# Sharing the last PSUM eviction of a block inversion between two engines, in a two-layer hybrid encoder

## The chip, the cores and the metric

The kernel runs on one core of a Trainium2 chip. The metric is the device time of one execution in microseconds (us). TensorE multiplies matrices into PSUM, VectorE and ScalarE read PSUM and work on SBUF, GpSimd does a few small powers, SyncE issues the DMAs.

## The reference, cut to what matters

Two layers, 256 tokens, width 2048. A layer is a norm, one input projection, two groups of heads, their gates, one output projection and a residual:

```
h = rms_norm(x); proj = h @ w_in
r, k, v, xw, xa = bidir_token_shift(...)      # 16 heads of 64, RWKV-7, two directions
S = S * w_t - (S kk_t) (a_t kk_t)^T + v_t k_t^T ;  y_t = S r_t     # per head, per direction
q, k_at, v_at -> rope -> windowed attention with a sink            # 16 query heads, 4 key heads
x = x + concat(y_rw * silu(g_rw), y_at * silu(g_at)) @ w_out
```

The change lies in the recurrence. The kernel computes it in chunks of 64 tokens. Inside a chunk the delta rule needs the inverse of a unit triangular 64 x 64 matrix for each head, direction and chunk.

## The kernel before, in words

**The weight stream.** The two projections are TensorE's bulk. Each weight tile is loaded as f32 (`raw`) and split by `wsplit` (line 217) into a high part `hi` (ScalarE, line 222) and the rest `lo` (VectorE, line 224), in two halves of 512 columns; three matmuls a step multiply them (`pm`, lines 292 to 294).

**Windows and slots.** `layer` (line 655) walks windows of 64 weight steps, each cut into 12 slots (`window`, line 394). At the head of each slot pieces of other work are put in, then the slot's 5 or 6 weight steps follow. The pieces are Python generators, one `yield` a piece. `scans` (line 1019) says which generator of which pair of heads advances at which slots:

- `scan_p` (line 690) prepares a pair: decays, keys, and a bonus `bv`. It has 13 pieces. `STAGE_P0` (line 47) gives the slots of the first pair, in windows 0 and 1; its last pieces come in window 2 by `STAGE_P[1]` (line 46), as for every pair.
- `scan_i` (line 776) builds a pair's chunk matrices and inverts them: matmuls `pg` for direction 0 and then 1, each masked by VectorE into `ge` (line 792) and copied in part to `AB` by ScalarE; `pt` (lines 807 and 815) and level 0 of the inversion (`pq`, line 886); five more levels (`pq`, `pd`, line 905, and VectorE's masked copy into `TC`, line 907); then a last correction. It takes all 12 slots of its window and slots 0 and 1 of the next.
- `scan_b` (line 938) runs the recurrence over the chunks, one or two windows later.

**The last correction.** `pf` (line 909) is a pair of PSUM banks. `turn` (line 860) puts the transposed columns of the last level into columns 256 to 383 of both banks; the matmuls of lines 914 to 919 put sums into columns 0 to 255. ScalarE copies the sums to `FN` (line 921) and the transposed columns to `TT` (the function `turned` that `turn` returns, line 867). A slot later `pn` (line 925) multiplies `FN` and `TT`.

**Buffers.** `pf`, `pg`, `pt`, `pq`, `pd`, `pn`, `pbn` and others are tiles of one pool of bank pairs, `ps_w`, with two buffers (line 151). `pf` of a pair stands in slot 0 of a window, and straight behind it come the two `pg` of the next pair.

**Order.** TensorE's order is the program's own (line 142). The order of the other engines is set when the program is built, by a list scheduler that goes by program position; `tc.high_priority(offset=n)` moves an instruction n places ahead (`PRIO_TC` is 400, line 59). `PA` and `PV` (line 239) are ScalarE and VectorE with program order kept among themselves.

In the trace the tiles have the names of their tags: `TC` is `tv`, `TT` is `tt`, `FN` is `q`, `GE` is `ge`, `BK` is `bk`.

Of the kernel before, what the change touches and what calls it, by code (L numbers as in the profile page):

```python
# [15 lines left out]
AF = mybir.ActivationFunctionType  # L16
# [5 lines left out]
T = 256  # L22
# [21 lines left out]
SLOTS = 12  # L44

STAGE_P = (([5], [3, 4, 5, 6, 7, 8, 9, 10, 11]), ([2], [0, 2]))
STAGE_P0 = (([], [10, 11]), ([2], [2, 4, 5, 7, 8, 9, 10, 11]))
STAGE_I = (list(range(SLOTS)), [0, 1])
STAGE_B = (list(range(1, 12)), [0, 1, 2, 3, 4, 5])
ATT = [  # L50
# [8 lines left out]
PRIO_TC = 400  # L59
# [75 lines left out]
def hybrid_trunk_kernel(ctx, tc, xT, wi, wv, wo, par, fing, dup, iup, sink, pos, cst, out):  # L135
    nc = tc.nc
    V, A, G, PE, SY = nc.vector, nc.scalar, nc.gpsimd, nc.tensor, nc.sync
# [15 lines left out]
    def wpair(name):  # L153

        return ps_w.tile([128, 2, 512], F32, tag="w", name=name)
# [4 lines left out]
    def st(tag, shape, dt=F32, bufs=1):  # L160
        return sp.tile([128, *shape], dt, tag=tag, name=tag, bufs=bufs)

    def pick(t, rows, off, *dims):

        a = t[rows]
        return bass.AP(tensor=a.tensor, offset=a.offset + off, ap=[a.ap[0], *dims])

    every = slice(0, 128)
# [486 lines left out]
    def layer(l):  # L655
# [120 lines left out]
        def scan_i(p, t):  # L776
# [75 lines left out]
            TT = st("tt", [2, NC, 64], F16)  # L852
# [7 lines left out]
            def turn(ps, b):  # L860

                for d, c, h in dch:
                    PE.matmul(
                        ps[half[h ^ d], d, c * 32 : (c + 1) * 32], hq(TC, d, c, h),
                        pick(EYE, half[h], (1 - d) * b, [2 * b, 32 // b], [1, b]), start=True, stop=True,
                    )
                return lambda: A.activation(  # L867
                    pick(TT, every, b, [T - b, 2], [2 * b, 128 // b], [1, b]), ps.rearrange("p d (n b) -> p d n b", b=b), AF.Copy
                )

            for li, b in enumerate(LEVELS):

# [22 lines left out]
                for d, c, h in dch:  # L895
                    PE.matmul(narrow(pq[:, d], h ^ d, c), hq(AB, d, c, h), sub(TC, h, d, c, d * b), start=True, stop=True)  # L896
                turned = li > 1 and turn(pq[:, :, 128:256], LEVELS[li - 1])

                A.activation(t_sub(QF), flat4(pq[:, :, 0:128]), AF.Copy)
# [8 lines left out]
                yield  # L908
            pf = wpair("pf")
            turned = turn(pf[:, :, 256:384], LEVELS[-1])  # L910
            o = lambda d, c, h: pf[half[h ^ d], d, c * 64 : (c + 1) * 64]
            for d in range(2):
# [5 lines left out]
                PE.matmul(o(d, c, h), hq(AB, d, c, h), hq(TC, d, c, h), start=False, stop=False, skip_group_check=True)  # L918
                PE.matmul(o(d, c, h), hq(AL, d, c, h), hq(TC, d, c, h), start=False, stop=True, skip_group_check=True)
            FN = st("q16", [2, NC, 64], F16)  # L920
            A.activation(FN.rearrange("p d c j -> p d (c j)"), pf[:, :, 0:T], AF.Copy)
            turned()
            yield

            pn = wpair("pn")
# [93 lines left out]
        def scans(w):  # L1019

            gens = []
            prep = [(w, STAGE_P0[w])] if w < 2 else [(2, STAGE_P[1]), (1, STAGE_P[0])]
            stages = [(lag, scan_p, at[0]) for lag, at in prep]
            stages += [(4, scan_b, STAGE_B[1]), (3, scan_i, STAGE_I[1]), (3, scan_b, STAGE_B[0])]
            stages += [(2, scan_i, STAGE_I[0])]
            stages += [(lag, scan_p, at[1]) for lag, at in prep]
            for lag, scan, at in stages:
                p = w - lag
                if 0 <= p < NP:
                    if (scan, p) not in chains:  # L1030
                        chains[scan, p] = scan(p, L.ts[p])
                    gens.append((chains[scan, p], at))
            return gens
# [210 lines left out]
```

## Time and profile before

| | us |
|---|---|
| median of 3 runs (lowest, highest) | 1191.46 (1190.85, 1194.27) |
| the profiled execution | 1191.11 |
| its span, first to last instruction | 1189.3 |
| TensorE matmuls busy | 1152.2 (97%) |
| VectorE busy | 910.1 (77%) |
| ScalarE busy | 792.6 (67%) |

All durations are of the one profiled execution. Engines: PE is TensorE (PEld its weight loads), DVE is VectorE, ACT is ScalarE, POOL is GpSimd, SP is SyncE. A row of the timeline has the start in us from the span's start, the duration, the engine, the line, the operation, what is written from what, the shape and a count; in brackets stand the engine's idle time before it and what ended it. The granted TensorE clock was 0.993 of full speed over the span.

### The profile page before, as it was taken

What the parts mean: (1) busy time and instruction counts of PE and PEld (TensorE: products, weight loads), DVE (VectorE), ACT (ScalarE), POOL (GpSimd) and SP (SyncE); (2) the same over time, 40 slices, a digit from 0 to 9 for tenths busy, and PEclk for the clock granted to TensorE, in tenths of its full rate; (3) what the DMA queues carried; (4) which work ended last, traced back from release to release, by engine and by line L of the source; (5) the groups of instructions that cost most, each with busy time, mean ns of one, the idle gap of its engine ahead of it and who ended that gap; (6) DMA issues with size and microseconds to landing.
All of it is one profiled execution on the core that took longest, in us unless ns stands there. A gap on an engine that the chain in (4) does not pass through costs nothing.

```text
span 1189.3 us, 38176 instructions
## 1 busy us (share of the span) xinstructions
PE 1152.2 (97%) x16151; PEld 1081.0 (91%) x16151; DVE 910.1 (77%) x2017; ACT 792.6 (67%) x1987; POOL 20.7 (2%) x23
## 2 busy tenths in 40 slices
PE   8999999999999999999999999999999999999996
PEld 6988988898898989899999888988898899989996
DVE  7889878988877678766678888878887767786554
ACT  6657776777777566655555777776777766765553
POOL 0000000000000000000000000000000000000000
PEclk9999999999999999999999999999999999999998
DMA  7553333333333434477654433333333344346663
GB/s 256 165 169 123 110 106 115 112 96 112 108 95 119 138 116 136 143 236 238 207 184 166 135 123 115 99 108 115 112 102 100 117 135 124 113 147 190 212 187 120
DMA packets 60410, 166.63 MB, mean 140 GB/s; under 512 B 7728, under 2 KB 22736, under 8 KB 60240
## 3 DMA queue, kind: packets, MB, share of 16 engines
q1 hardware_dynamic: 60240, 164.21, 43.1%
q8 instruction: 126, 2.06, 0.7%
q14 instruction: 44, 0.36, 0.1%
HBM read 157.37 MB, written 4.19 MB: 136 GB/s over the span
## 4 chain that ended last, share of the span: by engine, by line
PE 67%; issue 16%; DVE 7%; ACT 7%; DMA 2%; SPq 0%; POOL 0%; DVEq 0%; POOLq 0%; ACTq 0%
PE pm L292 17%; PE pm L293 14%; PE pm L294 14%; DVE lo L224 3%; ACT hi L222 2%; PE pcc L952 2%; PE pcc L978 2%; PE pg L786 1%; PE py L959 1%; DMA raw<-wi 1%; PE pq L896 1%; PE pd L905 1%; ACT ysq L996 1%; PE pcc L965 1%; PE py L985 1%
## 5 line engine op out<-in xcount | busy, mean ns | idle before, releaser
L292 PE MATMUL pm<-XH,hi 128*128 128x256 f32 x1664 | 490.7, 295 | 1.2 <-ACT XH L184 0.8
L294 PE MATMUL pm<-XH,lo 128*128 128x256 f32 x1664 | 468.3, 281 | 2.9 <-DVE lo L224 2.9
L293 PE MATMUL pm<-XL,hi 128*128 128x256 f32 x1664 | 467.7, 281 | 0.8 <-DVE XL L185 0.6
L224 DVE TENSOR_TENSOR lo<-raw,hi 128x512 fp32r<-128x512 f32 x560 | 368.6, 687 | 126.0 <-ACT hi L222 120.4
L222 ACT ACTIVATE hi<-raw 128x512 fp32r<-128x512 f32 x560 | 328.2, 624 | 187.9 <-PE pm L293 115.7
L292 PEld LDWEIGHTS pm<-XH,hi 128*128 128x128 f32 x1664 | 313.8, 189 | 13.2 <-ACT XH L184 1.6
L294 PEld LDWEIGHTS pm<-XH,lo 128*128 128x128 f32 x1664 | 313.9, 189 | 5.1 <-DVE lo L224 4.8
L293 PEld LDWEIGHTS pm<-XL,hi 128*128 128x128 f32 x1664 | 314.1, 189 | 1.4 <-DVE XL L185 1.4
L292 PE MATMUL pm<-MH,hi 128*128 128x256 f32 x512 | 144.0, 281 | 0.0
L293 PE MATMUL pm<-ML,hi 128*128 128x256 f32 x512 | 143.8, 281 | 0.0
L294 PE MATMUL pm<-MH,lo 128*128 128x256 f32 x512 | 143.8, 281 | 0.0
L292 PEld LDWEIGHTS pm<-MH,hi 128*128 128x128 f32 x512 | 96.6, 189 | 0.8 <-issue 0.8
L293 PEld LDWEIGHTS pm<-ML,hi 128*128 128x128 f32 x512 | 96.6, 189 | 0.0
L294 PEld LDWEIGHTS pm<-MH,lo 128*128 128x128 f32 x512 | 96.6, 189 | 0.0
L786 PE MATMUL pg<-mv,bk 64*128 64x128 f32 x512 | 36.6, 284 | 15.3 <-ACT tt L867 15.3
L786 PEld LDWEIGHTS pg<-mv,bk 64*128 64x128 f32 x512 | 30.9, 187 | 18.8 <-ACT tt L867 17.9
L237 ACT ACTIVATE AB<-ge 64x256 f16<-64x256 f32 x64 | 26.6, 416 | 29.3 <-DVE ge L792 28.6
L970 ACT ACTIVATE suv<-pcc 64x128 f32<-64x128 f32 x128 | 34.4, 269 | 12.4 <-PE pcc L968 7.6
L1063 ACT ACTIVATE mv<-mv,mx 128x257 f32<-128x257 f32 x64 | 31.9, 501 | 14.6 <-DVE mx L1060 14.6
L792 DVE TENSOR_TENSOR ge<-pg,C 128x1024 f32<-128x1024 f32 x32 | 38.7, 1221 | 1.8 <-PE pg L786 0.3
L907 DVE CAST_PREDICATED tv<-LV,pd 128x256 f16<-128x256 uint8 x80 | 34.5, 431 | 4.1 <-PE pd L905 2.8
L434 DVE TENSOR_TENSOR u<-pm,rb 128x256 f32<-128x256 f32 x52 | 21.1, 407 | 16.8 <-PE pm L294 16.7
(248 smaller groups left out, 1868.9 us busy)
## 6 DMA issues: line engine op xcount, KB each, us to landing
raw<-wi SPq DMA_DIRECT2D x207, 512.0 KB
raw<-wo SPq DMA_DIRECT2D x64, 512.0 KB
raw<-wv SPq DMA_DIRECT2D x8, 512.0 KB
rrot<-u SPq DMA_DIRECT2D x80, 32.0 KB
vg<-xT SPq DMA_DIRECT2D x16, 128.0 KB
xd<-vg SPq DMA_DIRECT2D x16, 128.0 KB
vg<-xd SPq DMA_DIRECT2D x16, 128.0 KB
g<-dup SPq DMA_DIRECT2D x16, 97.0 KB
```

What stands on the lines that cost most here:

```text
L222: A.activation(hi[:, q], raw[:, q], AF.Copy)
L224: V.tensor_tensor(lo[:, q], raw[:, q], hi[:, q].bitcast(F32), op=ALU.subtract)
L237: return lambda *a, **k: tc.keep_in_program_order(getattr(self.engine, name)(*a, **k))
L292: PE.matmul(pm, wh, rh[:, kk, :], start=(kk == 0), stop=False)
L293: PE.matmul(pm, wh, rl[:, kk, :], start=False, stop=False)
L294: PE.matmul(pm, wl, rh[:, kk, :], start=False, stop=(kk == 15))
L786: PE.matmul(pg[:, h, c * 128 : (c + 1) * 128], BK[half[h], d, c, 1 - h : 3 - h, :].rearrange("p s j -> p (s j)"), MV[half[h], d, c].rearra ...
L792: V.tensor_tensor(GEd(d), pg.rearrange("p h (c x) -> p h c x", c=NC), gm[d].unsqueeze(1).unsqueeze(1).to_broadcast([128, 2, NC, 128]), op= ...
L907: V.copy_predicated(t_sub(TC), t_mask, flat4(pd[:, :, 0:128]))
L952: PE.matmul(pc[half[h], 0, d, :], GE[h][r, d, ci[d], 0, :], SUV[r, d, ci[d], h, :], start=True, stop=True)
L970: A.activation(here(h), pc[half[h], 1], AF.Copy)
L1063: A.activation(Sc[:, h, q, 0:257], Sc[:, h, q, 0:257], AF.Exp, scale=0.125, bias=mx[:, q : q + 1], accum_out=den[:, q : q + 1])
```

## The change

Two edits. `turned` can now run on VectorE, and for the last correction it does. Both copies of VectorE, the transposed columns and the second half of the sums (direction 1, the second bank), stand in a block with priority offset 400; ScalarE copies the first half of the sums. The levels call `turned()` without the argument and keep ScalarE. Besides, the first pair's slot list for window 1 loses the entry 9; the pieces behind it each come at the next entry, and the last two in window 2.

```diff
-STAGE_P0 = (([], [10, 11]), ([2], [2, 4, 5, 7, 8, 9, 10, 11]))
+STAGE_P0 = (([], [10, 11]), ([2], [2, 4, 5, 7, 8, 10, 11]))
...
-                return lambda: A.activation(
-                    pick(TT, every, b, [T - b, 2], [2 * b, 128 // b], [1, b]), ps.rearrange("p d (n b) -> p d n b", b=b), AF.Copy
-                )
+                def turned(last=False):
+                    dst, src = pick(TT, every, b, [T - b, 2], [2 * b, 128 // b], [1, b]), ps.rearrange("p d (n b) -> p d n b", b=b)
+                    if last:
+                        V.tensor_copy(dst, src)
+                    else:
+                        A.activation(dst, src, AF.Copy)
+
+                return turned
...
             FN = st("q16", [2, NC, 64], F16)
-            A.activation(FN.rearrange("p d c j -> p d (c j)"), pf[:, :, 0:T], AF.Copy)
-            turned()
+            with tc.high_priority(offset=PRIO_TC):
+                turned(True)
+                V.tensor_copy(FN[:, 1].rearrange("p c j -> p (c j)"), pf[:, 1, 0:T])
+            A.activation(FN[:, 0].rearrange("p c j -> p (c j)"), pf[:, 0, 0:T], AF.Copy)
             yield
```

## Rows read from the trace of the kernel before

**Rows 1.** The page: busy us of each engine, share of the span, instructions.

```profile
PE 1152.2 (97%) x16151; PEld 1081.0 (91%) x16151; DVE 910.1 (77%) x2017; ACT 792.6 (67%) x1987; POOL 20.7 (2%) x23
```

**Rows 2.** TensorE's waits: who waited for whom, us in total, times, longest.

```profile
PE pg L786 <- ACT tt L867: 15.3, 14, 2.5
PE pbn L686 <- DVE ge L792: 4.1, 2, 2.1
...
PE pn L928 <- ACT tt L867: 0.4, 2, 0.2
```

**Rows 3.** Timeline of slot 0 of one window: start, duration, engine, line.

```profile
151.46 0.23 PE L919 MATMUL pf<-tv,AL 64*64 64x64 f16 x4
...
152.25 0.17 DVE L997 TENSOR_SCALAR yv<-yv 128x4 f32<-128x4 f32 x1 [0.26 <-ACT ysq L996]
152.40 0.64 ACT L222 ACTIVATE hi<-raw 128x512 fp32r<-128x512 f32 x1
...
152.56 0.43 DVE L447 SCALAR_TENSOR_TENSOR vg<-g 128x256 f32<-128x256 f32 x1
152.90 0.29 DVE L854 COPY tv<-EYE 128x512 f16<-128x512 f16 x1
152.92 0.61 ACT L921 ACTIVATE q<-pf 128x512 f16<-128x512 f32 x1
...
153.10 0.69 DVE L224 TENSOR_TENSOR lo<-raw,hi 128x512 fp32r<-128x512 f32 x1
...
153.40 0.41 ACT L867 ACTIVATE tt<-pf 128x256 f16<-128x256 f32 x1
153.70 2.59 DVE L792 TENSOR_TENSOR ge<-pg,C 128x1024 f32<-128x1024 f32 x2
...
153.86 1.16 PE L786 MATMUL pg<-mv,bk 64*128 64x128 f32 x16 [1.07 <-ACT tt L867]
...
157.18 0.27 PE L807 MATMUL pt<-C,vg 64*64 64x64 f32 x1
```

**Rows 4.** VectorE's groups by line and form: busy us, mean ns, idle before.

```profile
L571 DVE TENSOR_SCALAR VA<-pva,rt 128x256 f32<-128x256 f32 x2 | 0.8, 388 | 0.0
```

**Rows 5.** Timeline of the final norm.

```profile
1180.27 0.38 ACT L210 ACTIVATE rb<-pr 128x256 f32<-128x256 f32 x1 [2.60 <-PE pr L208]
1180.68 0.69 DVE L1161 TENSOR_TENSOR X<-X,pr 128x512 f32<-128x512 f32 x1 [1.41 <-ACT rb L210]
```

**Rows 6.** Timeline of slot 0 in two other windows.

```profile
112.91 1.16 PE L786 MATMUL pg<-mv,bk 64*128 64x128 f32 x16 [0.50 <-ACT tt L867]
...
362.77 0.17 DVE L997 TENSOR_SCALAR yv<-yv 128x4 f32<-128x4 f32 x1 [0.26 <-ACT ysq L996]
362.85 0.29 DVE L854 COPY tv<-EYE 128x512 f16<-128x512 f16 x1
```

**Rows 7.** Timeline: the level copies that start earliest and latest behind their matmuls.

```profile
93.16 0.45 DVE L907 CAST_PREDICATED tv<-LV,pd 128x256 f16<-128x256 uint8 x1 [0.35 <-PE pd L905]
...
225.50 0.30 PE L905 MATMUL pd<-QF,tt 64*64 64x32 f16 x16
...
227.85 0.42 DVE L907 CAST_PREDICATED tv<-LV,pd 128x256 f16<-128x256 uint8 x1
```

**Rows 8.** Timeline of the first layer's window 2, slots 0 and 1.

```profile
74.44 2.06 PE L786 MATMUL pg<-mv,bk 64*128 64x128 f32 x32
...
74.98 0.42 DVE L237 TENSOR_TENSOR th<-lw,th 128x256 fp32r<-128x256 f32 x1
...
78.55 0.48 PE L686 MATMUL pbn<-th,BONES 128*128 128x256 f32 x2 [2.05 <-DVE ge L792]
...
79.57 0.85 ACT L237 ACTIVATE AB<-ge 64x256 f16<-64x256 f32 x2 [0.28 <-DVE ge L792]
...
80.73 0.46 PE L807 MATMUL pt<-C,vg 64*64 64x64 f32 x16
...
81.64 0.33 PE L886 MATMUL pq<-tv,AB 64*64 64x32 f16 x10
```

## The prediction

> **What bounds the kernel now.** I read the page's busy shares first: the TensorE matmuls fill 97% of the span [rows 1]. So the end is set by TensorE's queue, and a change is worth what it takes out of TensorE's idle time (1189.3 - 1152.2 = 37.1 us) less what it puts in. The list of TensorE's waits, read next, says where that idle time lies [rows 2]: 15.3 us in 14 waits of `pg` (line 786) for ScalarE's copy at line 867, and 4.1 us in 2 waits of `pbn` (line 686) for VectorE's product `ge`. No other wait comes near. The change aims at these two. The 0.4 us of `pn` belongs to the first: same copy, in the two windows with no next pair.
>
> Then the timeline of one of the 14 places [rows 3]. The last matmul of the sums `pf` ends at 151.69. The program's next matmuls are `pg` for direction 0 (16, 1.16 us, they end at 152.78) and `pg` for direction 1. `pf` and both `pg` are bank pairs of a pool with two buffers, so the second `pg` needs `pf`'s buffer back. ScalarE gives it back: after a weight split (152.40, 0.64) it copies 512 sums (152.92, 0.61) and then the 256 transposed columns (153.40, 0.41, end 153.81); TensorE goes on at 153.86 after 1.07 us idle. The 14 gaps are nine of 1.07, two of 1.04, two of 0.50 [rows 6] and one of 2.50 (the longest in rows 2; ScalarE loads a table there): 15.3 us.
>
> **The eviction.** Removed from ScalarE: a copy of 512 and one of 256. Added: one of 256 (the first half of the sums) on ScalarE, two of 256 on VectorE, in the order transposed columns, second half. ScalarE's price for 256 from PSUM to half precision is its own row here, 0.41. VectorE has no such copy; the nearest row is line 571, PSUM to SBUF with one scalar, same size: 388 ns [rows 4]. From both sides: 0.29 (line 854's row, 512 elements that don't come from PSUM) and 0.43 (line 447's, two inputs) [rows 3]; I take 0.39.
>
> If VectorE gets to its copies early, ScalarE's own queue sets the time: its half still stands behind the weight split, 152.92 to about 153.32, and `pg` goes on at 153.37 instead of 153.86, 0.49 less. Where a gap is 1.07 or 1.04 or 2.50 this is the same piece (12 places, 12 x 0.49 = 5.9 us). Of the gap there remain 0.6 us, because the split stays in front. At the two 0.50 places [rows 6] at most 0.46 can go, and VectorE is busy there; I take 0.2 each, 0.4. The two waits of `pn` go: 0.4. Sum 6.7 us.
>
> A dependence hides in the edit: VectorE's transposed copy reads columns of both banks, ScalarE's half lies in one of them. At the kernel's end VectorE reads `pr` in PSUM, which it could do beside ScalarE's copy of the same columns to `rb`; it starts at 1180.68, 0.03 behind that copy's end, and the trace names the copy as its releaser [rows 5]. So ScalarE's half will wait for VectorE's first copy: its start is the later of 152.92 and that copy's end + 0.03.
>
> The Trainium skill (PSUM — Partial Sum Buffer, section "PSUM bank collisions raise a hardware error") says that two engines may not be in one bank and quadrant at the same time, not even to read, and that software has to order them. By that rule the three copies are not three parallel pieces but two behind one, which is the second case below, 1186.7 us, where VectorE is late. The wait in rows 5 agrees; no run yet shows it for these copies.
>
> Everything thus hangs on when VectorE's first copy starts. It gets a priority 400 places ahead, as line 907's copies have it. Of those, 80 in the trace, the earliest starts as soon as its matmuls let it (93.16, VectorE idle before it) and the latest 2.05 us behind them (225.80 to 227.85), with other VectorE work in between [rows 7], so that priority alone doesn't bring it to the front. Better evidence: `tv` at line 854 overwrites what the `pf` matmuls read, so whoever wrote the order held `pf` for done when `tv` was put in; and `tv` has low priority, yet it stands at 152.90, before the split's remainder `lo` at 153.10 [rows 3]. So the copy belongs at 152.90 at the latest, and, with its priority, before the product `vg` (152.56) if `pf` was held for done then. Where no `vg` stands there, `tv` follows `yv` directly (362.77, 362.85) [rows 6]. I take: directly behind `yv`, 152.34 to 152.73, second half to 153.04. ScalarE's half is then free from 152.76, before its 152.92.
>
> Behind the copies VectorE has `vg`, `tv`, `lo` and `ge`. They take on 0.7 us, less what VectorE stood idle between `yv` and `vg`: `ge` for direction 0 starts some 0.4 later, at 154.1, and the second `ge` ends at about 156.5, against 156.29. It frees the buffer for `pt` at line 807, which started at 157.18 [rows 3] and would now at 156.7. So of 0.9 us to spare about 0.2 is left, and I cost it at nothing; with that cover gone it costs TensorE, by the same rows, at most the 0.49 again.
>
> **The preparation.** The first pair's list loses slot 9, so in window 1 the steps behind it come one entry later: the bonus products (VectorE, 2) at 10, ScalarE's high part at 11, VectorE's low part in slot 0 of window 2 behind `pg`, the two `pbn` matmuls in slot 2 instead of slot 0, `bv` also in slot 2. None issues a DMA. Before, `pbn` stood straight behind the two `pg` (end 76.50) and waited for their buffer until VectorE's `ge` let it go: 78.55 [rows 8]. The wait goes in both layers, 4.1 us, and the next one is already there: TensorE would run 5 weight steps (15 matmuls at 0.117 in that trace, to 78.3), then `pt` (0.92, to 79.2), and `pq` at line 886 needs both directions' `AB`, done at 79.57 + 0.85 = 80.42, or 80.1 when the low part (0.42, 0.34 start to start) no longer stands before `ge`. Before, `pq` ran at 81.64 with 0.48 of `pbn` ahead of it, which now comes later. Gain: 81.64 - 80.1 - 0.48 = 1.05 a layer, 2.1 in all; bounds 0 (a new wait of `pbn` for a buffer in slot 2) and 4.1.
>
> **Sum.** 6.7 + 2.1 = 8.8 us off the profiled execution's 1191.11 (span 1189.3): 1182.3. That execution is 0.35 below the median of the runs, 1191.46; on the median: 1182.7 us.
>
> **Rivals.**
> - *VectorE late by one product.* The copy goes behind `vg`, in `tv`'s place: 152.90 to 153.29, ScalarE's half 153.32 to 153.72, `pg` at 153.77: only 0.09 gained. Nine such places 0.8, the two without `vg` and the one with the table load 0.5 each, 1.5, `pn` 0.4, preparation 2.1: 4.8 us, 1186.7. For it: the 80 copies of rows 7, most of which start behind an operation that began after the matmuls' end. Against: `tv` right behind `yv` where it could.
> - *Given back in the levels.* VectorE works 12.5 us more (32 x 0.39), and each window's five level copies run on it. If they and the `lo` halves come out in another order and TensorE waits about 0.4 us a window for them, the 6.7 are gone and some 1.5 us remain: 1190. For it: one order serves all the engines, and one edit can shift it. Against: TensorE hardly waits for VectorE today.
> - *Slower: the copy behind `lo`.* ScalarE's half waits for VectorE. With the first copy in the place of `ge`, 153.70 to 154.09, ScalarE's half runs 154.12 to 154.53 and `pg` goes on at 154.58, 0.72 later than now; 14 x 0.72 = 10.1, less 2.1 from the preparation: 8.0 more than now, 1199.5. It decides from a start at 152.98, 1.29 us behind the last sum: 0.39 + 0.03 + 0.41 + 0.05 is then the old 153.86. Against: `tv` before `lo`.
>
> **How the numbers follow.** Forecast 0.48, late by one product 0.22, given back 0.18, behind `lo` 0.12. Range 1180 to 1192: below, the preparation's upper bound (1180.7) with a little more at the two short gaps; above, the given-back case and somewhat more; the last rival is left out. The forecast's own range is 1180 to 1185. 0.3% (3.6 us) is about what a measurement of this kernel can tell from no change: faster means under 1187.9, slower over 1195.0. Faster: all of the forecast, most of the second case (0.15), a little of the third (0.04): 0.67. Slower: the last and a little of the third: 0.13. The rest, 0.20, is the same.
>
> **What would show it.** In the changed profile: TensorE's wait at `pg` falls from 15.3 to about 9 us with most single gaps near 0.6; VectorE's transposed copy directly behind `yv`, about 0.39 us long; ScalarE's half starting where the 512 did; the `pbn` wait gone and about 1 us before `pq` at line 886 in each layer's third window. It is wrong if VectorE's copy stands behind `vg` or `lo`, if the gap at `pg` is above 1 us, or if new waits for `tv` or `lo` appear.

## The result: 3.6 us slower, and the profile after

The changed kernel takes 1195.05 us (median of 20 runs, 1192.04 to 1199.15) against 1191.40 (20 runs, 1189.96 to 1194.45) for the kernel before: the ratio is 1.0028, with an interval of 1.0017 to 1.0038. That is slower by about what a measurement of this kernel can tell, and the interval does not reach 1. Forecast were 1182.7 us and a range of 1180 to 1192: the sign was wrong. The profiled execution took 1194.82 us with a span of 1192.8.

The page's busy line of the changed kernel; its columns are those of [rows 1]:

```profile
PE 1154.1 (97%) x16151; PEld 1081.3 (91%) x16151; DVE 920.0 (77%) x2049; ACT 786.9 (66%) x1971; POOL 20.7 (2%) x23
```

VectorE has its 32 copies more, ScalarE 16 fewer, and TensorE does the same work: the moved load is there as planned. What it brought is in TensorE's waits of the changed kernel (us in total, times, longest):

```profile
PE pg L786 <- ACT q L929: 19.4, 14, 2.8
...
PE pq L891 <- ACT AB L237: 1.0, 4, 0.2
PE pt L807 <- DVE ge L792: 0.8, 2, 0.4
```

Beside [rows 2]: the wait for the eviction rose from 15.3 to 19.4 us instead of falling to about 9. The two waits of `pbn` (4.1) are gone, and so are those of `pn` (0.4); `pt` and `pq` wait instead. The 14 gaps at `pg` were nine of 1.07, two of 1.04, two of 0.50 and one of 2.50. They are now nine of 1.40, two of 0.83, one of 0.88, one of 1.39 and one of 2.83.

The same place as in [rows 3], in the timeline of the changed kernel (the last sum ends at 152.61; lines after 867 have moved: 870 is the copy of the transposed columns, 928 and 929 are the halves of the sums):

```profile
152.38 0.23 PE L924 MATMUL pf<-tv,AL 64*64 64x64 f16 x4
...
153.33 0.64 ACT L222 ACTIVATE hi<-raw 128x512 fp32r<-128x512 f32 x1
153.48 0.43 DVE L447 SCALAR_TENSOR_TENSOR vg<-g 128x256 f32<-128x256 f32 x1
153.83 0.42 DVE L870 CAST tt<-pf 128x256 f16<-128x256 f32 x1
154.16 0.41 DVE L928 CAST q<-pf 128x256 f16<-128x256 f32 x1
154.49 0.68 DVE L224 TENSOR_TENSOR lo<-raw,hi 128x512 fp32r<-128x512 f32 x1
154.67 0.39 ACT L929 ACTIVATE q<-pf 128x256 f16<-128x256 f32 x1 [0.70 <-DVE q L928]
155.09 0.29 DVE L854 COPY tv<-EYE 128x512 f16<-128x512 f16 x1
155.11 0.71 PE L786 MATMUL pg<-mv,bk 64*128 64x128 f32 x8 [1.40 <-ACT q L929]
```

Two things are to be seen. VectorE's first copy runs behind `vg`, 1.22 us behind the last sum; it stands where `tv` stood. It is so at ten of the 14 places: the nine with a gap of 1.40 and the one with 2.83, where ScalarE loads a table. And ScalarE, free at 153.97, starts its half only at 154.67, 0.10 behind the end of VectorE's *second* copy, and the trace names that copy as its releaser. The forecast had ScalarE wait for the first copy alone.

At the two places without a `vg` the copy did come directly behind `yv`, as forecast (timeline of the changed kernel; the last sum ends at 364.86):

```profile
365.43 0.17 DVE L1004 TENSOR_SCALAR yv<-yv 128x4 f32<-128x4 f32 x1 [0.26 <-ACT ysq L1003]
365.50 0.42 DVE L870 CAST tt<-pf 128x256 f16<-128x256 f32 x1
365.84 0.41 DVE L928 CAST q<-pf 128x256 f16<-128x256 f32 x1
366.35 0.38 ACT L929 ACTIVATE q<-pf 128x256 f16<-128x256 f32 x1 [0.16 <-DVE q L928]
366.78 0.94 PE L786 MATMUL pg<-mv,bk 64*128 64x128 f32 x12 [0.83 <-ACT q L929]
```

Here too ScalarE waits for the second copy, and the gap is 0.83 us, not 0.6. So even where the order was right the three copies run in series, and over half of the forecast gain is gone: the gap fell from 1.04 to 0.83, by 0.21 us instead of 0.49.

One of the two formerly short gaps (0.50 in [rows 6]) has the same shape, with `lo` ahead of the copies. In the timeline of the changed kernel ScalarE was idle 0.74 us before its half:

```profile
112.88 0.41 DVE L928 CAST q<-pf 128x256 f16<-128x256 f32 x1
...
113.39 0.38 ACT L929 ACTIVATE q<-pf 128x256 f16<-128x256 f32 x1 [0.74 <-DVE q L928]
...
113.82 1.16 PE L786 MATMUL pg<-mv,bk 64*128 64x128 f32 x16 [0.88 <-ACT q L929]
```

The gaps add up: 9 x 0.33 - 2 x 0.21 + 0.33 + (0.38 + 0.89) = 4.1 us more. The preparation gave 0.6 a layer back (below, `stage_only`), the two `pn` waits 0.4. The first 32 weight steps, ahead of any changed work, were 0.9 us longer in this execution than in the one of before; that start differs from execution to execution (1.15 longer in `stage_only`, 0.7 in `evict_only`) and is no effect of the change. 4.1 - 0.4 - 1.2 + 0.9 = 3.4, against 3.5 between the spans.

### The profile page after: what moved, and what is told of

Same layout as the page of the kernel before. It is cut to its first block, busy times and chain, and to the rows that moved or that the text cites. A ratio compares the mean times of both kernels' runs of the same rounds, so it can differ in the third digit from the quotient of the medians.

```text
span 1192.8 us, 38192 instructions
## 1 busy us (share of the span) xinstructions
PE 1154.1 (97%) x16151; PEld 1081.3 (91%) x16151; DVE 920.0 (77%) x2049; ACT 786.9 (66%) x1971; POOL 20.7 (2%) x23
## 4 chain that ended last, share of the span: by engine, by line
PE 68%; issue 16%; DVE 9%; ACT 5%; DMA 2%; SPq 0%; POOL 0%; DVEq 0%; POOLq 0%; ACTq 0%
PE pm L292 17%; PE pm L294 14%; PE pm L293 14%; DVE lo L224 3%; PE pcc L959 2%; PE pcc L985 2%; PE py L966 1%; PE pg L786 1%; ACT hi L222 1%; DMA raw<-wi 1%; PE pq L901 1%; PE pd L910 1%; PE pcc L972 1%; PE py L992 1%; ACT ysq L1003 1%
## 5 line engine op out<-in xcount | busy, mean ns | idle before, releaser
L786 PE MATMUL pg<-mv,bk 64*128 64x128 f32 x512 | 37.2, 286 | 19.4 <-ACT q L929 19.4
L977 ACT ACTIVATE suv<-pcc 64x128 f32<-64x128 f32 x128 | 34.5, 269 | 12.2 <-PE pcc L975 7.6
L987 DVE TENSOR_TENSOR suv<-pcc,pc 64x128 f32<-64x128 f32 x96 | 27.4, 286 | 8.5 <-PE pcc L985 6.9
```

The source lines that it names most:

```text
L786: PE.matmul(pg[:, h, c * 128 : (c + 1) * 128], BK[half[h], d, c, 1 - h : 3 - h, :].rearrange("p s j -> p (s j)"), MV[half[h], d, c].rearra ...
L977: A.activation(here(h), pc[half[h], 1], AF.Copy)
L987: V.tensor_tensor(here(h, i + 1), pS[half[h]], pick(PC, half[h], i, [2 * NC - 1 - 2 * i, 2], [0, 64]), op=ALU.mult)
```

## The experiments

The account that I formed from the two traces: the loss is the eviction's alone. It has two parts. The order puts VectorE's first copy behind `vg` at most places, and all three copies of one `pf` run one behind the other, whichever engine has them. The rivals: the preparation lost the time; only copies that share a bank are put in series; the place in the queue is harmless and VectorE's slower copying does it. Every experiment was timed against the kernel before on its chip.

**One part alone: `evict_only`.** The eviction as changed, the preparation's list as before.

```diff
-STAGE_P0 = (([], [10, 11]), ([2], [2, 4, 5, 7, 8, 10, 11]))
+STAGE_P0 = (([], [10, 11]), ([2], [2, 4, 5, 7, 8, 9, 10, 11]))
```

> The eviction edit alone, the first pair's slots as before. Theory A (the three copies run one after another, and at most places VectorE's first copy stands behind the product vg): the same gaps at pg as in the changed kernel, 19.4 us in 14 waits against 15.3, the two pn waits (0.4) gone, the pbn waits of 4.1 us back; about 3.8 us slower than before, 1195. Theory B (the loss comes from the slot edit, or from VectorE's added work in the levels): the time of before or faster, within 1 us of 1191, and the gaps at pg no longer than before.

Measured: 1196.20 us, ratio 1.0046 (1.0033 to 1.0059). TensorE's waits in its trace:

```profile
PE pg L786 <- ACT q L929: 19.4, 14, 2.8
PE pbn L686 <- DVE ge L792: 4.1, 2, 2.0
```

The eviction alone makes the kernel slower, with the same 19.4 us at `pg`; the old `pbn` wait is back.

**The other part alone: `stage_only`.** The kernel before with the changed list, and nothing else.

```diff
-STAGE_P0 = (([], [10, 11]), ([2], [2, 4, 5, 7, 8, 9, 10, 11]))
+STAGE_P0 = (([], [10, 11]), ([2], [2, 4, 5, 7, 8, 10, 11]))
```

> The slot edit alone, ScalarE evicts as before. Theory A: the pbn waits (4.1 us in two layers) go, but pt and pq then wait for ge and AB, which come later because ScalarE's high part of the bonus, late by a slot, stands before the weight split; net gain 0.5 to 0.7 us a layer, 1.2 us in all, 1190. The forecast's own reckoning, if only the eviction was wrong: 2.1 us, 1189.3. Theory B: slower than before by over 2 us.

Measured: 1190.97 us, ratio 0.9995 (0.9984 to 1.0006): no change that can be told. Its trace shows why the 4.1 us of `pbn` did not become a gain. The window of [rows 8], in the timeline of `stage_only`:

```profile
75.57 2.06 PE L786 MATMUL pg<-mv,bk 64*128 64x128 f32 x32
75.72 0.48 DVE L237 SCALAR_TENSOR_TENSOR lw<-lw,PR,kr 128x256 f32<-128x256 f32 x1
76.23 0.42 ACT L237 ACTIVATE th<-lw 128x256 fp32r<-128x256 f32 x1 [2.24 <-DVE lw L237]
76.55 1.13 ACT L222 ACTIVATE hi<-raw 128x512 fp32r<-128x512 f32 x2
77.19 1.29 DVE L224 TENSOR_TENSOR lo<-raw,hi 128x512 fp32r<-128x512 f32 x2 [0.67 <-ACT hi L222]
78.74 2.35 DVE L792 TENSOR_TENSOR ge<-pg,C 128x1024 f32<-128x1024 f32 x2
80.02 0.46 PE L807 MATMUL pt<-C,vg 64*64 64x64 f32 x16 [0.41 <-DVE ge L792]
```

Three rows of the timeline of the kernel before, where this `pg` started at 74.44 [rows 8]:

```profile
74.49 0.42 ACT L237 ACTIVATE th<-lw 128x256 fp32r<-128x256 f32 x1 [1.64 <-DVE lw L237]
74.82 1.14 ACT L222 ACTIVATE hi<-raw 128x512 fp32r<-128x512 f32 x2
...
77.18 2.35 DVE L792 TENSOR_TENSOR ge<-pg,C 128x1024 f32<-128x1024 f32 x2
```

There too ScalarE's high part `th` waited for VectorE's product `lw`, and the weight split `hi` stood behind it. One entry later, `lw` ends 0.63 us behind the start of `pg`; ScalarE sits idle 2.24 us for it, and `th` starts 0.66 us behind `pg` instead of 0.05. So `hi`, `lo` and `ge` are late one after the other: `ge` starts 3.17 us behind `pg` (78.74 - 75.57; 2.74 in the kernel before), and `pt` waits 0.41 us for it (`pq` then 0.25 and 0.24 for `AB`). Aligned by the weight steps of the two traces, TensorE is 2.4 us ahead at this window's start and has lost 1.8 and 1.9 of it by the window's end: net about 0.6 a layer.

**Another entry dropped: `stage_last`.** The kernel before with entry 11 left out of the list instead of 9, so that `th` and the bonus products keep their slots.

```diff
-STAGE_P0 = (([], [10, 11]), ([2], [2, 4, 5, 7, 8, 9, 10, 11]))
+STAGE_P0 = (([], [10, 11]), ([2], [2, 4, 5, 7, 8, 9, 10]))
```

> The kernel before, with the last entry (11) of the first pair's list dropped instead of entry 9: only VectorE's low part and the pbn matmuls come later, the bonus products and ScalarE's high part stay. Theory A (in the changed kernel ScalarE's high part, a slot later, held up the weight split and with it ge): without that, ge starts earlier, no wait at pt, the gain is the forecast's 1.05 us a layer, 2.1 in all against 1.2 of the slot edit; 1189. Rival: the weight split wasn't it, pt waits as long as there, 1.2 us or less.

Measured: 1188.68 us, ratio 0.9970 (0.9959 to 0.9982). The same stretch in its timeline:

```profile
75.23 2.06 PE L786 MATMUL pg<-mv,bk 64*128 64x128 f32 x32
75.28 0.42 ACT L237 ACTIVATE th<-lw 128x256 fp32r<-128x256 f32 x1 [1.65 <-DVE lw L237]
...
77.80 2.35 DVE L792 TENSOR_TENSOR ge<-pg,C 128x1024 f32<-128x1024 f32 x2
79.18 0.46 PE L807 MATMUL pt<-C,vg 64*64 64x64 f32 x16
```

`th` starts 0.05 us behind `pg`'s start instead of 0.66, `ge` 2.57 instead of 3.17, and `pt` no longer waits. In the trace this is worth 0.9 to 1.2 us in the first layer and 1.2 to 1.5 in the second, depending on the weight step at which the two traces are laid together, 2.3 or 2.4 in all: what the prediction wanted from the changed list (2.1). The timed runs give 3.6 us, with an interval from 2.1 to 4.9. The wait that the prediction overlooked was that of `th` for a later `lw`, with `hi` behind it on ScalarE.

**The order alone: `vg_later`.** The changed kernel with the product `vg` issued three weight steps later, so that VectorE's copies stand ahead of it; `vg` and the copies are kept in program order (`PV`).

```diff
-        def silu_evac(place):
+        def silu_evac(place, late=False):
...
-                V.scalar_tensor_tensor(place(), th, 1.0, g, op0=ALU.add, op1=ALU.mult)
+                vg = lambda e: e.scalar_tensor_tensor(place(), th, 1.0, g, op0=ALU.add, op1=ALU.mult)
+                S.later(3, lambda: vg(PV)) if late else vg(V)
...
-            inproj(5 + 4 * p, silu_evac(new(t, "gr", "vg", 8)))
+            inproj(5 + 4 * p, silu_evac(new(t, "gr", "vg", 8), late=True))
...
-                        V.tensor_copy(dst, src)
+                        PV.tensor_copy(dst, src)
...
-                V.tensor_copy(FN[:, 1].rearrange("p c j -> p (c j)"), pf[:, 1, 0:T])
+                PV.tensor_copy(FN[:, 1].rearrange("p c j -> p (c j)"), pf[:, 1, 0:T])
```

> The changed kernel with the product vg of the first gate put behind VectorE's two copies. Theory A: VectorE's transposed copy now follows yv at all typical places, as it does in the one place without vg of the changed kernel (gap 0.83): the gaps at pg fall from 1.40 to 0.83 at nine places, the sum at pg from 19.4 to about 13.5 us, and the time by about 6 us to 1189. ScalarE's half still starts 0.10 behind VectorE's second copy, not at 1.23 us behind the last sum. Theory B (VectorE's load, not its order): the gaps or the levels' waits keep the time within 2 us of the changed kernel's 1195.

Measured: 1187.20 us, ratio 0.9968 (0.9955 to 0.9980). Its timeline where `vg` used to stand, and its wait:

```profile
152.52 0.42 DVE L237 CAST tt<-pf 128x256 f16<-128x256 f32 x1
152.85 0.41 DVE L237 CAST q<-pf 128x256 f16<-128x256 f32 x1
153.36 0.38 ACT L930 ACTIVATE q<-pf 128x256 f16<-128x256 f32 x1
153.80 1.05 PE L787 MATMUL pg<-mv,bk 64*128 64x128 f32 x14 [0.83 <-ACT q L930]
```

```profile
PE pg L787 <- ACT q L930: 13.4, 14, 2.0
```

With `vg` out of the way the gap is 0.83, as at the two places without one, and 6.0 us of `pg`'s wait are gone against the changed kernel. So the order is the larger part of the loss. The edit also takes `vg` from in front of `ge` in the first pair's window: `pt` no longer waits there (0.8 us in the changed kernel), a small part of the gain that has nothing to do with the eviction. The series remains: ScalarE starts 0.10 behind the end of VectorE's second copy here too, and the gap stays above the forecast's 0.6.

**Are only shared banks put in series? `bank_split`.** ScalarE takes everything of direction 0 (one bank), VectorE everything of direction 1 (the other), so that no two engines read the same bank.

```diff
-                        V.tensor_copy(dst, src)
+                        for d, copy in ((0, lambda o, i: A.activation(o, i, AF.Copy)), (1, V.tensor_copy)):
+                            copy(FN[:, d].rearrange("p c j -> p (c j)"), pf[:, d, 0:T])
+                            copy(pick(TT, every, T if d else b, [2 * b, 128 // b], [1, b]), src[:, d])
...
-                V.tensor_copy(FN[:, 1].rearrange("p c j -> p (c j)"), pf[:, 1, 0:T])
-            A.activation(FN[:, 0].rearrange("p c j -> p (c j)"), pf[:, 0, 0:T], AF.Copy)
```

> The changed kernel with the eviction split by bank: ScalarE copies the sums and the transposed columns of the first bank, VectorE those of the second, so that no bank is read by two engines. Theory A (engines that read one PSUM tile, the pair of banks, are put in series whatever the bank): VectorE's copies start about 0.1 us behind ScalarE's second copy, pg goes on about 2.7 us behind the last sum, gaps near 1.6 at the typical places, 3 us or more slower than the changed kernel. Rival C (only a shared bank puts them in series): they run side by side, pg goes on at about 1.95, gaps near 0.85, some 5 us faster than the changed kernel.

Measured: 1203.32 us, ratio 1.0107 (1.0090 to 1.0124), the slowest of all. Timeline of `bank_split` (the last sum ends at 155.77) and its wait:

```profile
157.00 0.40 ACT L870 ACTIVATE q<-pf 128x256 f16<-128x256 f32 x1
157.18 0.69 DVE L224 TENSOR_TENSOR lo<-raw,hi 128x512 fp32r<-128x512 f32 x1
157.27 0.30 ACT L870 ACTIVATE tt<-pf 128x128 f16<-128x128 f32 x1
157.79 0.42 DVE L871 CAST q<-pf 128x256 f16<-128x256 f32 x1
158.12 0.28 DVE L872 CAST tt<-pf 128x128 f16<-128x128 f32 x1
158.55 0.71 PE L786 MATMUL pg<-mv,bk 64*128 64x128 f32 x8 [1.68 <-DVE tt L872]
```

```profile
PE pg L786 <- DVE tt L872: 24.4, 14, 3.1
```

VectorE's copies come behind ScalarE's second one (157.79, after an end at 157.57), with `lo` ahead of them. VectorE was not idle there, so this row alone shows a place in the queue and no wait; in the built program VectorE's first copy does wait for the count that ScalarE's second copy posts, though they read different banks and write different tiles (`FN` and `TT`). The two engines also share these output tiles; in a program in which each of the four copies writes a tile of its own, built and not run, the wait is the same. So here it is neither the bank nor a shared output that orders the copies, but the tile `pf`: the program puts accesses of two engines to one `pf` in the order of its text. The Trainium skill (PSUM — Partial Sum Buffer, section "PSUM bank collisions raise a hardware error") asks for an order only within one bank and quadrant. By that rule the copies of `bank_split` could run side by side; here they did not, so that rule is not what binds. A `pf` made of two separately tracked tiles was not tried, since all eight banks are taken as the kernel is laid out; whether its copies would run side by side stays open.

**Change of engine or place? `dve_all`.** The changed kernel with all copies of `pf` on VectorE: the sums as one copy of 512, nothing on ScalarE.

```diff
-                V.tensor_copy(FN[:, 1].rearrange("p c j -> p (c j)"), pf[:, 1, 0:T])
-            A.activation(FN[:, 0].rearrange("p c j -> p (c j)"), pf[:, 0, 0:T], AF.Copy)
+                V.tensor_copy(FN.rearrange("p d c j -> p d (c j)"), pf[:, :, 0:T])
```

> The changed kernel with both halves of the sums copied by VectorE, behind the transposed columns; ScalarE reads nothing of pf. It takes away the change of engine, not the place behind vg. Theory A: transposed columns from 1.21 us behind the last sum, 512 sums from 1.55 to 2.25, pg goes on at about 2.3: gaps near 1.2 where the changed kernel has 1.40 and the kernel before 1.07; the sum at pg about 16.4 us, some 3 us faster than the changed kernel, 1192. Rival (VectorE's load decides): slower than the changed kernel, since VectorE works more.

Measured: 1194.34 us, ratio 1.0011 (1.0002 to 1.0021). Its wait at `pg` is 17.8 us. Two rows of its timeline:

```profile
155.00 0.68 DVE L928 CAST q<-pf 128x512 f16<-128x512 f32 x1
155.83 0.38 PE L786 MATMUL pg<-mv,bk 64*128 64x128 f32 x2 [1.28 <-DVE q L928]
```

The gap is 1.28 us, 0.12 shorter than with ScalarE's half split off. So the split across engines, meant to save time, costs 0.12 of the 0.33 a place. The other 0.21 is VectorE's own: it starts its copies hardly earlier behind the last sum (1.21 us) than ScalarE did (152.92 - 151.69 = 1.23 in [rows 3]), and it needs 0.34 + 0.68 + 0.15 = 1.17 from there to `pg`, where ScalarE needed 153.86 - 152.92 = 0.94. I had expected a gap of 1.2 and a sum of 16.4 us. The difference between this kernel and the changed one is read from the traces: the intervals of their ratios overlap.

**Hiding the wait instead: `fill2` and `fill3`.** The kernel before with two (or three) of slot 0's weight steps put between the old pair's `pf` and the new pair's `pg`. TensorE works while ScalarE copies; the copies stay as they were.

```diff
+FILL = 2
...
+                if g is None:
+                    if i == 0:
+                        S.run(at)
+                        done += at
+                    continue
...
+                    if scan is scan_i and lag == 2 and p > 0:
+                        gens.append((None, FILL))
```

> The kernel before, with two of slot 0's five weight steps moved between the pf matmuls and the next pair's pg; all else as before. If the gap at pg is nothing but the time that pf's eviction takes, TensorE fills it: two steps are 0.70 us, the gaps fall from 1.07 to about 0.37, some 9.4 us over the 14 places, 1181.6. The margins of pt and pq behind pg shrink by two steps and should just hold. Rival: the wait comes back at pt (for ge) or pq (for AB) in the next slot, and less than 3 us remain.

Measured: 1187.29 us, ratio 0.9952 (0.9941 to 0.9964). TensorE's waits in the trace of `fill2`:

```profile
PE pq L892 <- ACT vf L940: 3.4, 14, 0.4
...
PE pg L792 <- ACT tt L873: 3.1, 10, 1.6
```

The 15.3 us at `pg` fell to 3.1, but `pq` now waits for ScalarE's copy of `pn` at 14 places. Of the 9.4 us expected 5.8 came, less than the 12.2 that went at `pg` minus the 3.4 that came at `pq`. Laid together by their weight steps, the two traces show why: where the gap was 1.07, a window gains about 0.43 us. The wait at `pg` falls by 0.90 (1.07 to 0.17), the one listed at `pq` takes 0.22, and most of the rest goes between `pf` and `pg`: the two steps, counted at 0.70, hold the first `pg` back by 0.91 (it starts at 155.16 with the last sum's end at 154.32; before, at 151.62 with 151.69). The two windows with a gap of 0.50 gain nothing. A part of the timeline of `fill2` shows the new wait:

```profile
159.83 0.60 ACT L940 ACTIVATE vf<-pn 128x512 f32<-128x512 f32 x1
160.48 0.33 PE L892 MATMUL pq<-tv,AB 64*64 64x32 f16 x11 [0.22 <-ACT vf L940]
```

> The same with three steps (1.05 us): the gap at pg near 0, but pt would start 4.35 us behind the last sum and ge ends at 4.65, so a new wait of about 0.3 a window; about the same time as with two steps, 1181. Rival as there.

Measured: 1192.42 us, ratio 0.9996 (0.9988 to 1.0005). Its waits:

```profile
PE pq L892 <- ACT vf L940: 9.7, 14, 0.7
...
PE pg L792 <- ACT tt L873: 1.2, 1, 1.2
```

One step more takes another 1.9 us from `pg` and gives 6.3 to `pq`: the gain is gone. I had named `pt` and `ge` as the next wait; it was `pq` and `vf`. So two steps (0.70 us) are worth putting in this place, and a third is not.

**Together: `fill2_last`, `fill1_last`, `vg_last`, `vg_fill2_last`.** `fill2_last` is `fill2` with the list of `stage_last`; `fill1_last` the same with `FILL = 1`; `vg_last` is `vg_later` with that list; `vg_fill2_last` has `vg_last`'s edits and two filling steps.

```diff
-STAGE_P0 = (([], [10, 11]), ([2], [2, 4, 5, 7, 8, 9, 10, 11]))
+STAGE_P0 = (([], [10, 11]), ([2], [2, 4, 5, 7, 8, 9, 10]))
+FILL = 2
```

> Both single edits that helped, on the kernel before: two weight steps between pf and pg, and entry 11 dropped from the first pair's list; ScalarE evicts. They lie in different places, so their gains should add: 0.48% and 0.30%, about 1184 where the kernel before has 1193, ratio 0.992. Rival: the first pair's window has no pf and the two overlap in nothing, so only a new order of VectorE and ScalarE could eat it; then no better than 0.995.

> One weight step between pf and pg, entry 11 dropped, ScalarE evicts. The gap at pg falls by one step, from 1.07 to 0.72, without the new wait of pq: 14 x 0.35 = 4.9 us and the slots' 2.4 to 3.6: ratio 0.993 to 0.994, between no step and two.

> The eviction by both engines with VectorE's copies before vg, and entry 11 dropped instead of 9. Theory A: the three copies in series end 0.24 us a window earlier than ScalarE's two did, 13.4 us at pg instead of 15.3, and the first pair's pt and pq wait less: ratio 0.995 to the kernel before, 0.002 better than with entry 9 dropped.

> The same with two weight steps between pf and pg. Theory A: the eviction then hides behind the two steps (its end 1.87 us behind the last sum, the first pg would end at 1.86), so the gap at pg is near 0 where two steps alone leave 0.17, and what is left is the wait of pq for the copy of pn, 0.2 a window. Some 2 us better than two steps with ScalarE's eviction at most, ratio 0.990 to 0.993.

| kernel | median us | ratio | interval | wait at `pg`, us | `pq` for `vf`, us |
|---|---|---|---|---|---|
| `fill2_last` | 1182.78 | 0.9919 | 0.9901 to 0.9936 | 3.1 | 3.3 |
| `vg_fill2_last` | 1183.79 | 0.9926 | 0.9910 to 0.9942 | 1.6 | 6.7 |
| `fill1_last` | 1185.08 | 0.9937 | 0.9918 to 0.9956 | 7.7 | none |
| `vg_last` | 1186.98 | 0.9950 | 0.9934 to 0.9967 | 13.4 | none |

`fill2_last` beats both kernels, with the old eviction on ScalarE. Moving copies to VectorE on top of it takes 1.5 us from `pg` and adds 3.4 at `pq`; the intervals of the two overlap, so no difference between them can be told.

## Why the prediction was wrong, point by point

- **What bounds the kernel: right.** TensorE's waits decided. The changes at `pg`, `pn`, `pbn`, `pt` and `pq`, with the start's 0.9 us, account for the difference between the spans.
- **The price of VectorE's copy: right within 0.03.** Forecast 0.39 us within 0.29 to 0.43; measured 0.42 for the transposed columns and 0.41 for the half. Back to back they start 0.33 apart.
- **Where VectorE's first copy starts: the first step that failed.** "Directly behind `yv`" held at the two places without `vg`; at ten it stood behind `vg`, the place that the first rival named with 0.22 for nine of them; at the two formerly short gaps it stood behind `lo`. My inference from `tv` was half right: the copy took `tv`'s place but did not pass `vg`. The copies of [rows 7] had warned that a priority alone does not do it. `vg_later`, which takes `vg` away, brings the start to the forecast's place and the gap from 1.40 to 0.83. That whoever wrote the order took `vg` before it held `pf` for done is argued, not shown.
- **What ScalarE's half waits for: the second step that failed. It took both to change the sign.** The prediction saw from [rows 5] that an order is put on two engines' reads of one bank pair, but let ScalarE wait for the first copy alone ("its start is the later of 152.92 and that copy's end + 0.03"). In the trace it waits for VectorE's last copy and 0.10 us more, though the second copy reads only the other bank. In the built program the first copy posts no count of its own, so a wait for it is a wait for the second's; and by `bank_split` the tile alone would have put the wait there. Which of the two does it here is not told apart. By the rival's sum, late copies with ScalarE waiting for the first alone would have gained 0.09 us a place; early copies in series gained 0.24 (1.07 to 0.83 in `vg_later`); late and in series they lost 0.33. With the series the rival's own sum would have been a loss: one behind the other are 0.33 + 0.41 + 0.10 + 0.39 + 0.05 = 1.28 from the first copy's start, 153.83 to 155.11, where the kernel before needs 0.94 from ScalarE's first copy to `pg` (152.92 to 153.86 in [rows 3]).
- **So the rival "late by one product" had the right place and the wrong price.** It gave +0.09 us a place; measured was -0.33. The slower rival had a right mechanism, ScalarE waiting for VectorE, but put VectorE's start behind `lo`, and its point of decision (a start 1.29 us behind the last sum) assumed one copy to wait for. By the measured steps `pg` comes 1.28 behind the first copy's start, and in the kernel before it came 153.86 - 151.69 = 2.17 behind the last sum: the point lies at 2.17 - 1.28 = 0.89, and the nine places start at 1.22.
- **The short gaps: wrong sign.** Forecast 0.2 less at each of the two; measured 0.38 and 0.89 more. The prediction said that VectorE is busy there and still counted a gain.
- **The preparation: mechanism half right, size off.** `pbn`'s wait of 4.1 us went, but the gain was about 0.6 a layer in the trace, not 1.05, since `th` waited longer for `lw` and held up `hi`, `lo` and `ge` behind it; the timed run of that part alone shows no change. My count of what the entry moves listed "ScalarE's high part at 11" and did not follow it along ScalarE's queue. `stage_last`, where it stays, gives the forecast's size or more.
- **Given back in the levels: did not happen.** TensorE's wait for `tv` is 0.2 us in all in the changed kernel; VectorE had the time.

## What to carry to other kernels

Before an eviction is split across engines, look at what the program makes wait for what: copies from one tile can be put in series whichever banks they read, and a waiter can be released by a later instruction than the one it needs, so that three short pieces on two engines end after two longer ones on one. A moved instruction must be followed down the queue of its own engine as well as to its consumer: what it is now in front of is late by its wait as well as by its length. And where the producer cannot be made faster, a little of TensorE's other work between the two can hide the wait, here 12 of 15.3 us, until the next consumer becomes the one that waits; the right amount is found by steps, not by adding all that fits.

## What the runs showed of the hardware that I had not expected

The long gap at `pg` (2.50 us, where ScalarE loads a table) may cost a second time. In the profiled execution of the kernel before, TensorE's granted clock was 0.50 (1.2 GHz) in a stretch shortly behind that gap, which ended at 321.21; in `stage_only`, behind the same gap of 2.50, it stayed at 1.00 (2.4 GHz). The windows view of each (columns: us, busy us and count of PE, PEld, DVE, ACT and POOL, granted clock, DMA share, GB/s), the kernel before first:

```profile
322.60:326.00 3.40, 3.40 (x35) 3.14 (x35) 2.99 (x5) 1.37 (x4) 0.00 (x0) 0.50 0.32 124
```

```profile
322.00:328.00 6.00, 6.00 (x116) 5.56 (x117) 5.19 (x10) 4.02 (x10) 0.00 (x0) 1.00 0.26 90
```

By the two traces, laid together by their weight steps, this cost the kernel before about 1.5 us in that execution. The other traces go the same way without settling it: of the ten whose gap here is 1.9 to 3.1 us, eight have such a stretch behind it and two (`stage_only` and `stage_last`, both 2.50) have none; the four whose gap is 1.6 us or less have none here. But four traces also have one at about 80 us, and others later, so this gap is not the only place. The changed kernel and the kernel before each have this one, so it is not what makes the difference between them; the execution of `bank_split` had four (at 83, 329, 373 and 674 us). Runs of one kernel spread over some 3 to 7 us where ten or more were taken, and such stretches may be a part of it; that was not tested. So a span of one execution can't judge an edit that is worth a microsecond or two.
